# Query, key and value projection by seven block products of eight, with the gate kept in device memory

## The chip, the cores and the metric

The kernel runs on one core of one Trainium2 chip. The metric is the time of one execution on the device in microseconds (us). The kernel before takes 1717.29 us, the median of 3 runs (1715.92 to 1720.21). One execution was recorded by the hardware profiler, and its span is 1717.7 us; all durations below come from that execution.

The engines of a core run their own instruction streams in order: PE (TensorE) multiplies matrices, DVE (VectorE) and ACT (ScalarE) work on rows of numbers, POOL (GpSimd) does odd jobs, SP (SyncE) here only issues transfers between device memory and the core's memory (DMA). An instruction waits where it stands for what it needs, and all behind it on its engine wait with it.

## The reference

Two layers over 512 tokens of width 2048, each with a normalisation in front that is modulated by a conditioning vector, a gate by that vector behind, and a residual sum. Layer 0 mixes tokens by windowed means; layer 1 is sparse attention. What the change touches is layer 1:

```
proj = h @ w_in                                  # (512, 2048) @ (2048, ...)
q, k, v, gate, qi, ki, wi = split(proj)          # q, k, v, gate: 16 heads x 128
q, k = rope(q), rope(k)                          # the first 32 of each head's 128
sel = top_k(relu(qi . ki) weighted by wi, 128)   # keys kept for each query, causal
p = softmax(q . k / sqrt(128), over sel)
out = ((p @ v) * silu(gate)) @ w_out
```

All is float32. For that accuracy each matrix product is made of three products of shorter floats: an operand is split into a high part (hi, wh) and the rest (lo, wl), and hi·wh + hi·wl + lo·wh is summed.

## The kernel before

Layer 1 goes through four stages. The index projection (weights `widx`) gives qi, ki and wi; the gate projection (`wgate`) gives the gate, and in the same stretch DVE finds the top 128 keys; then come 16 heads one after the other with `wqkv`; then the output projection (`wout1`), the residual sum and the last norm.

Weights come in units of two blocks of 128 rows. `unit()` issues the load on SP (L130, 3 buffers `st`), ACT makes the high part `wh` from it (L132), and DVE subtracts to get the rest `wl` (L134), which is the last reading of the buffer. Units are made some steps ahead of use. Two helpers multiply: `gemm_t` (L177 to L179, weights stationary, 512 columns of tokens) and `gemm_n` (L199 to L201, tokens stationary, the weights' 384 columns of one head's q, k and v streaming).

The loop over heads (L732 to L737) makes for each head 8 units x 4 token tiles x 2 blocks x 3 products = 192 matmuls of 384 columns. ACT copies the four results out of PSUM into `nat` (L735). The attention of a head is cut into items (`head_items`): rotation of q and k, transposes and splits of q and k, four rows of logits with a running maximum on DVE (L697), exp on ACT (L700), normalising on DVE (L701, L702), transposes and splits of p, and p @ v with the gate multiplied in (L727). These items wait in a queue `bg`; `step()` takes some after each weight unit of the next head, so that PE never runs out of work. A scheduler settles the order of each engine from the order of the code and its own estimates, and the order is fixed at build time.

The silu of the gate stays in the core's memory as 16 tiles `y` (L651). After the last head `y_split` splits them for the output projection. In the middle of the output projection `cond_rows` runs a second time (L242 to L250): it loads the conditioning row, spreads it over 128 partitions by four matmuls with a column of ones in plain float32 (L248), and ACT takes silu of it (L249) into `cb`; DVE multiplies it with rows of `modT` (L212) for the layer's gate.

Of the kernel before, what the change touches and what calls it, by code (L numbers as in the profile page):

```python
# [17 lines left out]
D = 2048  # L18
# [16 lines left out]
NC = 1  # L35
TWO_PI = 6.283185307179586
# [15 lines left out]
def trunk(ctx, tc, xT, cols, crow, pos, modT, win, wgrp, wout0, widx, wgate, wqkv, wout1, out):  # L52
# [5 lines left out]
    wp = ctx.enter_context(tc.tile_pool(name="wp", bufs=2))  # L58
    tp = ctx.enter_context(tc.tile_pool(name="tp", bufs=1))
    dp = ctx.enter_context(tc.tile_pool(name="dp", bufs=1, space=DRAM))  # L60
    ps = ctx.enter_context(tc.tile_pool(name="ps", bufs=1, space=PSUM))
    turn = [0]

    def bank4():
        return ps.tile([128, 512], F32, name="acc", tag="acc", bufs=4)

    def att():
        return ps.tile([128, 512], F32, name="att", tag="att", bufs=3)

    def misc():  # L70
        return ps.tile([128, 512], F32, name="misc", tag="misc", bufs=1)
# [5 lines left out]
    def tmp(shape=(128, 528)):  # L77
        return tp.tile(list(shape), F32, name="tmp", tag="tmp", bufs=4)

# [12 lines left out]
    acc = cp.tile([128, T], F32, name="acc")  # L92
    rbc = cp.tile([128, T], F32, name="rbc")
# [34 lines left out]
    def unit(src, w):  # L128
        st = wp.tile([128, 2, w], F32, name="st", tag="st", bufs=3)
# [7 lines left out]
    # every weight unit in the order of use; units are split ahead of their use  # L137
# [9 lines left out]
    plan += [(wqkv[h, kp], 384) for h in range(HEADS) for kp in range(8)]  # L147
    plan += [(wout1[c, kp], 512) for c in (0, 1, 2, 3, 3) for kp in range(8)]
# [14 lines left out]
    # out^T[m] (4 column tiles) += W[k, m]^T r[k], weights stationary  # L163
# [22 lines left out]
    # natural-layout projection: out[t, cols] for the given row tiles  # L186
# [66 lines left out]
    def norm_r(t0, t1):  # L253
        nb = (t1 - t0) // 128
        p = misc()
        for j in range(nb):
            mm(p[:, j:j + 1], acc[:, t0 + j * 128:t0 + j * 128 + 128], ones[:, 0:1], start=True, stop=True)
        s = tp.tile([128, 4, 4], F32, name="nrm", tag="nrm", bufs=2)
# [285 lines left out]
    for tt, o in early:  # L544
        n = o.shape[-1]
        nc.scalar.copy(inat[:, tt, 0:n], o)
# [304 lines left out]
```

## Time and profile before

| quantity | value |
|---|---|
| median of 3 runs | 1717.29 us |
| span of the profiled execution | 1717.7 us |
| PE busy | 1684.1 us, 98% of the span |
| DVE busy | 1098.1 us, 64% |
| ACT busy | 642.3 us, 37% |
| POOL busy | 23.9 us, 1% |
| read from and written to device memory | 283.74 MB, 8.39 MB |
| mean granted TensorE clock | 0.996 |

A busy share is the part of the span in which an engine had an instruction under way. The profile's text gives one line for a group of instructions with the line of the program, the engine, what is written and what is read, and the mean length of one. A timeline gives a start and a length of each; the time from one start to the next on the same engine is its pitch, which can be shorter than the length, since the end of an instruction overlaps with the start of the next.

### The profile page before, as it was taken

How to read it: one execution, taken by the hardware profiler on the slowest of the kernel's cores; microseconds unless marked ns; L12 is line 12 of the kernel's file. 1: busy time of each engine (PE TensorE's matmuls, PEld its weight loads, DVE VectorE, ACT ScalarE, POOL GpSimd, SP SyncE). 2: the span in 40 equal slices, each digit the busy share in tenths (PEclk: the TensorE clock that was granted, in tenths of full speed). 3: DMA queues.
4: the chain of work that ended last, by engine and by line, in shares of the span. 5: the costliest groups of instructions: out<-in, count | busy, mean ns of one | idle time of the engine just before them, and what ended most of it. 6: DMA issues, size and time to landing. Idle time of an engine off the chain costs nothing.

```text
span 1717.7 us, 23658 instructions
## 1 busy us (share of the span) xinstructions
PE 1684.1 (98%) x9284; PEld 1531.4 (89%) x9284; DVE 1098.1 (64%) x1867; ACT 642.3 (37%) x1024; POOL 23.9 (1%) x130
## 2 busy tenths in 40 slices
PE   4999999999999999999999999999999999999998
PEld 3888888888889999988889999999999999987897
DVE  6899998999855784566943444444444444554954
ACT  4622221344224563444223333333333333543334
POOL 1000000000000000110000000000000000000000
PEclk9999999999999999999999999999999999999999
DMA  8888988544867865432222222222222222226955
GB/s 327 319 302 308 332 331 324 185 145 172 322 206 249 248 213 172 148 99 74 96 88 88 80 83 83 83 76 81 83 78 81 82 83 83 85 86 226 354 185 178
DMA packets 82772, 293.68 MB, mean 171 GB/s; under 512 B 9314, under 2 KB 17634, under 8 KB 70370
## 3 DMA queue, kind: packets, MB, share of 16 engines
q1 hardware_dynamic: 82660, 292.17, 49.9%
q8 instruction: 73, 1.20, 0.3%
q14 instruction: 39, 0.32, 0.1%
HBM read 283.74 MB, written 8.39 MB: 170 GB/s over the span
## 4 chain that ended last, share of the span: by engine, by line
issue 89%; PE 9%; POOL 1%; DVE 1%; DMA 0%; ACT 0%; POOLq 0%; DVEq 0%; ACTq 0%; SPq 0%
PE acc L177 1%; PE acc L179 1%; PE acc L178 1%; PE acc L200 1%; PE acc L199 1%; PE acc L201 1%; PE att L199 1%; PE att L200 1%; PE att L201 1%; PE att L609 0%; PE att L610 0%; PE misc L583 0%; DVE wl L134 0%; DMA st<-widx 0%; DVE tmp L293 0%
## 5 line engine op out<-in xcount | busy, mean ns | idle before, releaser
L132 ACT CAST wh<-st 128x1024 fp32r<-128x1024 f32 (+2 forms) x360 | 342.9, 953 | 835.7 <-PE acc L178 319.8
L134 DVE TENSOR_TENSOR wl<-st,wh 128x1024 fp32r<-128x1024 f32 (+2 forms) x360 | 396.6, 1102 | 342.4 <-ACT wh L132 336.9
L199 PE MATMUL acc<-wh,hi 128*128 128x384 f32 (+2 forms) x1120 | 381.6, 341 | 0.0
L201 PE MATMUL acc<-wh,lo 128*128 128x384 f32 (+2 forms) x1120 | 373.7, 334 | 0.0
L200 PE MATMUL acc<-wl,hi 128*128 128x384 f32 (+2 forms) x1120 | 373.3, 333 | 0.0
L177 PE MATMUL acc<-hi,wh 128*128 128x512 f32 (+1 forms) x842 | 310.0, 369 | 0.0
L178 PE MATMUL acc<-lo,wh 128*128 128x512 f32 (+1 forms) x842 | 309.5, 368 | 0.0
L179 PE MATMUL acc<-hi,wl 128*128 128x512 f32 (+1 forms) x842 | 309.2, 367 | 0.0
L212 DVE SCALAR_TENSOR_TENSOR ms<-ms,cb 128x2048 f32<-128x2048 f32 x96 | 218.9, 2285 | 23.0 <-ACT cb L249 12.3
L199 PEld LDWEIGHTS acc<-wh,hi 128*128 128x128 f32 x1120 | 210.6, 188 | 0.6
L200 PEld LDWEIGHTS acc<-wl,hi 128*128 128x128 f32 x1120 | 210.7, 188 | 0.3 <-DVE wl L134 0.2
L201 PEld LDWEIGHTS acc<-wh,lo 128*128 128x128 f32 x1120 | 210.3, 188 | 0.0
L178 PEld LDWEIGHTS acc<-lo,wh 128*128 128x128 f32 x842 | 158.9, 189 | 26.6
L177 PEld LDWEIGHTS acc<-hi,wh 128*128 128x128 f32 x842 | 159.1, 189 | 26.4
L179 PEld LDWEIGHTS acc<-hi,wl 128*128 128x128 f32 x842 | 158.8, 189 | 26.4 <-DVE wl L134 0.4
L177 PE MATMUL att<-hi,wh 128*128 128x512 f32 (+1 forms) x374 | 138.3, 371 | 2.2 <-ACT hi L298 2.2
L178 PE MATMUL att<-lo,wh 128*128 128x512 f32 (+1 forms) x374 | 138.4, 370 | 0.0
L179 PE MATMUL att<-hi,wl 128*128 128x512 f32 (+1 forms) x374 | 138.3, 370 | 0.0
L697 DVE CUSTOM_DVE_ANT_0 lg<-att,mbias 128x256 f32<-128x256 f32 (+2 forms) x48 | 26.8, 558 | 95.2 <-PE att L694 95.2
L177 PEld LDWEIGHTS att<-hi,wh 128*128 128x128 f32 x374 | 70.9, 190 | 16.2 <-ACT hi L298 2.6
L178 PEld LDWEIGHTS att<-lo,wh 128*128 128x128 f32 x374 | 71.2, 190 | 12.5 <-DVE lo L299 0.8
L179 PEld LDWEIGHTS att<-hi,wl 128*128 128x128 f32 x374 | 71.3, 191 | 11.6
(208 smaller groups left out, 1969.4 us busy)
## 6 DMA issues: line engine op xcount, KB each, us to landing
ms<-modT SPq DMA_DIRECT2D x96, 1024.0 KB, 7.0
st<-wqkv SPq DMA_DIRECT2D x128, 384.0 KB, 3.0
st<-wout SPq DMA_DIRECT2D x88, 512.0 KB, 4.2
st<-win SPq DMA_DIRECT2D x64, 512.0 KB, 5.1
st<-wgate SPq DMA_DIRECT2D x40, 512.0 KB, 3.5
st<-widx SPq DMA_DIRECT2D x32, 368.0 KB, 3.3
x<-xT SPq DMA_DIRECT2D x16, 256.0 KB, 5.5
st<-wgrp SPq DMA_DIRECT2D x8, 512.0 KB, 3.5
```

Of the source, the lines that this page charges most:

```text
L132: nc.scalar.copy(wh, st)
L134: nc.vector.tensor_tensor(wl, st, wh.bitcast(F32), op=OP.subtract)
L177: mm(o, wh[:, kk, ms], rh[:, t0:t1], start=first, stop=False)
L178: mm(o, wh[:, kk, ms], rl[:, t0:t1], start=False, stop=False)
L179: mm(o, wl[:, kk, ms], rh[:, t0:t1], start=False, stop=last)
L199: mm(o, hi[:, ts], wh[:, kk, 0:n], start=kp == 0 and kk == 0, stop=False)
L200: mm(o, hi[:, ts], wl[:, kk, 0:n], start=False, stop=False)
L201: mm(o, lo[:, ts], wh[:, kk, 0:n], start=False, stop=kp == 7 and kk == 1)
L212: nc.vector.scalar_tensor_tensor(st, st, 1.0, cell["cb"], op0=OP.mult, op1=OP.mult, accum_out=dst)
L697: nc.vector.tensor_tensor_reduce(out=lg, in0=o, in1=mbias[qb], scale=1.0, scalar=GONE, op0=OP.add, op1=OP.max, accum_out=st[:, 0:1])
```

## The change

For a pair of heads a = 2j and b = 2j+1 the product of tokens and weights is cut into 2 x 2 x 2 blocks: token halves (256 each), halves of the depth (1024 each), and the two heads. The eight block products become seven, after Strassen, in Winograd's form, with sums of blocks on both sides. Each product takes four slots; a slot has one unit of weights, two token tiles and 12 matmuls. A pair has 28 slots with 336 matmuls, where it had 384. The order in a pair is P1, P5, P6 four times in turn, then P3, P7 four times, then P2, P4 four times (`qplan`).

The sums on the token side are made once: S1, S2 and S4 by `s_item` (8 items, which the scheduler places in the index projection's stretch), S3 by `s3_item` in place in the first slots of the first pair. The sums on the weights' side are made for each pair by DVE (`q_unit`): 16 more subtractions of 128 x 768 in a pair. The loads have four buffers `qst` and are issued 2 units ahead of the split, which is 3 slots ahead of use; a pair has 24 loads, where it had 16, since head b's eight blocks are loaded twice (for P5 and P7, and for P6 and P3). The results leave PSUM by ACT for P1 and P2, and by 10 additions of 128 x 384 a pair on DVE for the other products.

The attention items are 11 per head now and one is taken per slot; q, k and v tiles have one buffer each. Head 14's items run in the first part of the output projection. The memory for the sums is found by writing each gate tile to device memory (`yd`), reading it back per head (`yg`), writing the product back for heads 0 to 13, and reading that for `y_split`. The second `cb` comes by one transfer that repeats the row on all partitions.

```diff
+QLOOK = 3
+QST = 4
+QAHEAD = 2
...
-    plan += [(wqkv[h, kp], 384) for h in range(HEADS) for kp in range(8)]
-    plan += [(wout1[c, kp], 512) for c in (0, 1, 2, 3, 3) for kp in range(8)]
...
+    yd = dp.tile([KT, 128, T], F32, name="yd")
...
+    HK = KT // 2
+    SS = {(i, k): (sp.tile([128, 256], F32R, name=f"s{i}h{k}"), sp.tile([128, 256], F32R, name=f"s{i}l{k}"))
+          for i in (1, 2, 4) for k in range(HK)}
+
+    def whole(dst, k):
+        hi, lo = hT[k]
+        nc.vector.tensor_tensor(dst, hi.bitcast(F32), lo.bitcast(F32), op=OP.add)
+
+    def s_item(k):
+        def run():
+            ha = yp.tile([128, T], F32, name="ha")
+            hb = yp.tile([128, T], F32, name="hb")
+            whole(ha, k)
+            whole(hb, k + HK)
+            s1, s2, s4 = (yp.tile([128, 256], F32, name=f"sf{i}") for i in (1, 2, 4))
+            nc.vector.tensor_tensor(s1, ha[:, 256:T], hb[:, 256:T], op=OP.add)
+            nc.vector.tensor_tensor(s2, s1, ha[:, 0:256], op=OP.subtract)
+            nc.vector.tensor_tensor(s4, hb[:, 0:256], s2, op=OP.subtract)
+            for i, t in ((1, s1), (2, s2), (4, s4)):
+                split(*SS[i, k], t)
+        return run
+
+    bg.extend(s_item(k) for k in range(HK))
...
+                y_tile(mt)
             nc.scalar.activation(y[mt][:, t0:T], o, AF.Silu)
+            nc.sync.dma_start(yd[mt], y[mt])
...
+    qplan = []
+    for j in range(HEADS // 2):
+        a, b = 2 * j, 2 * j + 1
+        for kp in range(4):
+            qplan += [("P1", kp, (a, kp)), ("P5", kp, (b, kp)), ("P6", kp, (b, 4 + kp))]
+        for kp in range(4):
+            qplan += [("P3", kp, (b, 4 + kp)), ("P7", kp, (b, kp))]
+        for kp in range(4):
+            qplan += [("P2", kp, (a, 4 + kp)), ("P4", kp, None)]
...
+    def q_loads(n):
+        while qpos[0] < min(n, len(qplan)):
+            src = qplan[qpos[0]][2]
+            if src:
+                st = wq.tile([128, 2, QW], F32, name="qst", tag="qst", bufs=QST)
+                nc.sync.dma_start(st, wqkv[src[0], src[1]])
+                qraw[qpos[0]] = st
+            qpos[0] += 1
+
+    def q_unit():
+        i = qpos[1]
+        qpos[1] += 1
+        q_loads(i + 1 + QAHEAD)
+        prod, kp, _ = qplan[i]
+        st = qraw.pop(i, None)
+        sub = lambda o, x, z: nc.vector.tensor_tensor(o, x, z, op=OP.subtract)
+        if prod == "P5":
+            sub(st, st, was["b11"])
+        elif prod == "P6":
+            t2[kp] = wq.tile([128, 2, QW], F32, name=f"t2_{kp}")
+            sub(t2[kp], st, was["t1"])
+            st = t2[kp]
+        elif prod == "P7":
+            sub(st, was["b22"], st)
+        elif prod == "P4":
+            sub(t2[kp], was["b21"], t2[kp])
+            st = t2[kp]
+        keep = {"P1": "b11", "P5": "t1", "P3": "b22", "P2": "b21"}.get(prod)
+        if keep:
+            was[keep] = st
+        wh = wq.tile([128, 2, QW], F32R, name="qwh", tag="qwh", bufs=QLOOK + 1)
+        wl = wq.tile([128, 2, QW], F32R, name="qwl", tag="qwl", bufs=QLOOK + 1)
+        split(wh, wl, st)
+        qready.append((wh, wl))
...
+    def q_slot(prod, kp, banks, wh, wl):
+        opens = prod in ("P1", "P5", "P6")
+        for tt in range(2):
+            o = banks[role[prod]][tt][:, 0:QW]
+            for kk in range(2):
+                hi, lo = lhs(prod, 2 * kp + kk, tt)
+                first = opens and kp == 0 and kk == 0
+                last = kp == 3 and kk == 1
+                mm(o, hi, wh[:, kk, :], start=first, stop=False, skip_group_check=not opens)
+                mm(o, hi, wl[:, kk, :], start=False, stop=False, skip_group_check=not opens)
+                mm(o, lo, wh[:, kk, :], start=False, stop=last, skip_group_check=not opens)
...
+    def s3_item(k):
+        def run():
+            ha = ap.tile([128, T], F32, name="lg", tag="lg", bufs=3)
+            whole(ha, k)
+            nc.vector.tensor_tensor(ha[:, 0:256], ha[:, 0:256], ha[:, 256:T], op=OP.subtract)
+            hi, lo = hT[k]
+            split(hi[:, 256:T], lo[:, 256:T], ha[:, 0:256])
+        return run
+
+    bg.extend(s3_item(k) for k in range(HK))
...
+            cell["y"] = ap.tile([128, T], F32, name="yg", tag="yg", bufs=2)
+            nc.sync.dma_start(cell["y"], yd[h])
...
+            nc.vector.tensor_tensor(cell["y"], o, cell["y"], op=OP.mult)
+            y[h] = cell["y"]
+            if h < HEADS - 2:
+                nc.sync.dma_start(yd[h], cell["y"])
...
-    for h in range(HEADS):
-        nat = ap.tile([128, 4, 384], F32, name="nat", tag="nat", bufs=1)
-        gemm_n(384, (0, 1, 2, 3), bank4,
-               lambda tt, o, nat=nat: nc.scalar.copy(nat[:, tt, :], o), nstep=1)
-        drain()
-        bg.extend(head_items(h, nat))
...
     def y_split(k):
+        src = y[k]
+        if k < HEADS - 2:
+            src = ap.tile([128, T], F32, name="yr", tag="lg", bufs=3)
+            nc.sync.dma_start(src, yd[k])
         yT[k] = hslots(k)
-        split(yT[k][0], yT[k][1], y[k])
-
-    for k in range(KT - 1):
-        y_split(k)
-    bg.append(lambda: y_split(KT - 1))
+        split(yT[k][0], yT[k][1], src)
...
+    for j in range(HEADS // 2):
+        a, b = 2 * j, 2 * j + 1
+        banks = {}
+        na = nb = None
+        for u in range(28):
+            while len(qready) < QLOOK + 1 and qpos[1] < len(qplan):
+                q_unit()
+            wh, wl = qready.popleft()
+            prod, kp, _ = qplan[28 * j + u]
+            if role[prod] not in banks:
+                r = role[prod]
+                banks[r] = [P["ps"].tile([128, 512], F32, name="b" + r, tag="b" + r, bufs=2) for _ in range(2)]
+            q_slot(prod, kp, banks, wh, wl)
+            if kp == 3:
+                B = [t[:, 0:QW] for t in banks[role[prod]]]
+                if prod == "P1":
+                    na = ap.tile([128, 4, QW], F32, name="na", tag="na")
+                    nb = ap.tile([128, 4, QW], F32, name="nb", tag="nb")
+                for tt in range(2):
+                    if prod == "P1":
+                        nc.scalar.copy(na[:, tt, :], B[tt])
+                        nc.scalar.copy(na[:, 2 + tt, :], B[tt])
+                    elif prod == "P5":
+                        ev(nb[:, 2 + tt, :], B[tt], na[:, tt, :], op=OP.add)
+                    elif prod == "P6":
+                        ev(nb[:, tt, :], B[tt], na[:, tt, :], op=OP.add)
+                    elif prod == "P3":
+                        ev(nb[:, tt, :], B[tt], nb[:, tt, :], op=OP.add)
+                    elif prod == "P7":
+                        ev(nb[:, 2 + tt, :], B[tt], nb[:, 2 + tt, :], op=OP.add)
+                    elif prod == "P2":
+                        nc.scalar.copy(na[:, tt, :], B[tt])
+                    else:
+                        ev(na[:, 2 + tt, :], B[tt], na[:, 2 + tt, :], op=OP.add)
+                if prod == "P7":
+                    bg.extend(head_items(b, nb))
+                    if j == HEADS // 2 - 1:
+                        hot.extend(lambda k=k: y_split(k) for k in range(HK))
+                elif prod == "P4":
+                    bg.extend(head_items(a, na))
+            step(1)
+    while hot:
+        hot.popleft()()
+    hot.extend(lambda k=k: y_split(k) for k in range(HK, HEADS - 2))
+    for k in (HEADS - 2, HEADS - 1):
+        bg.append(lambda k=k: y_split(k))
...
-    gemm_t(range(8), lambda k: yT[k], bank4, lambda m, o: early.append((m, o)), nstep=2)
+    gemm_t(range(8), lambda k: yT[k], bank4, lambda m, o: early.append((m, o)), nstep=2.6, nhot=2, mid={6: drain})
...
-    bg.append(lambda: cond_rows(op_, lambda: op_.tile([1, D], F32, name="cr", tag="ms", bufs=3)))
+    cell["cb"] = op_.tile([128, D], F32, name="cb")
+    nc.sync.dma_start(cell["cb"], crow.to_broadcast([128, D]))
+    nc.scalar.activation(cell["cb"], cell["cb"], AF.Silu)
```

The first place is DVE in the stretch of a head's logits. Before, with `wl` the rest of a weight unit, `lg` the logits of one row block and `stt` its maximum and sum:

```order
L134 TENSOR_TENSOR wl_9793<-st_9789,wh_9791 128x768
L161 TENSOR_TENSOR ql_9771<-att_9765,qh_9770 128x512
L161 TENSOR_TENSOR kl_9780<-att_9774,kh_9779 128x512
L697 ISA lg_9823,stt_9824<-att_9819,dmask_5868 128x128
L697 ISA stt_9824 128x1
L134 TENSOR_TENSOR wl_9834<-st_9830,wh_9832 128x768
L699 TENSOR_SCALAR stt_9824<-stt_9824 128x1
```

And now, in a pair in the middle, with `qwl` the rest of a unit, `qst` a loaded unit and `t2` a sum of units:

```order
L177 TENSOR_TENSOR qwl_10256<-qst_10201,qwh_10255 128x768
L760 TENSOR_TENSOR qst_10332<-qst_10332,qst_10305 128x768
L177 TENSOR_TENSOR ql_10250<-att_10244,qh_10249 128x512
L177 TENSOR_TENSOR qwl_10282<-t2_2_9844,qwh_10281 128x768
L177 TENSOR_TENSOR kl_10277<-att_10271,kh_10276 128x512
L760 TENSOR_TENSOR t2_0_10434<-qst_10362,qst_10332 128x768
L177 TENSOR_TENSOR qwl_10308<-qst_10253,qwh_10307 128x768
L854 ISA lg_10327,stt_10328<-att_10323,dmask_5869 128x128
L854 ISA stt_10328 128x1
L177 TENSOR_TENSOR qwl_10336<-t2_3_9929,qwh_10335 128x768
L856 TENSOR_SCALAR stt_10328<-stt_10328 128x1
```

Between the split of q and the maximum of the first logits there stood nothing but k's split; now two splits of units and one difference of units stand there too, and the difference reads `qst_10362`, a load that has to be in place by then.

The second place is SP between the gate's stage and the heads. Before:

```order
L130 DMA st_7882<-wgate 128x1024
L130 DMA st_7918<-wgate 128x1024
L130 DMA st_7956<-wqkv 128x768
L130 DMA st_7992<-wqkv 128x768
L130 DMA st_8040<-wqkv 128x768
```

And now, with `yst` a gate tile in the core and `yd` the gate in device memory:

```order
L712 DMA yd_114<-yst_8185 128x512
L712 DMA yd_114<-yst_8194 128x512
L712 DMA yd_114<-yst_8203 128x512
L842 DMA yg_8771<-yd_114 128x512
L712 DMA yd_114<-yst_8212 128x512
L842 DMA yg_9102<-yd_114 128x512
L750 DMA qst_8234<-wqkv 128x768
L750 DMA qst_8236<-wqkv 128x768
```

The first loads for the heads stood in the queue right behind the last of the gate's weights; now they stand behind the writes of the gate's last four tiles. `qst_8234` takes the memory of earlier tiles and waits, among others, for the write of `yst_8203`.

The third place is PE in the output projection. Before, with `cr` the conditioning row and `ones` the column of ones:

```order
L178 MATMUL acc_14143<-lo1_13678,wh_14033 128x512
L179 MATMUL acc_14143<-hi1_13677,wl_14035 128x512
L248 MATMUL acc_14153<-cr_14150,ones_73 128x512
L248 MATMUL acc_14156<-cr_14150,ones_73 128x512
L248 MATMUL att_14159<-cr_14150,ones_73 128x512
L177 MATMUL att_14122<-hi2_13681,wh_14063 128x512
```

A part of the difference between the two streams on PE:

```order
-L248 MATMUL acc<-cr,ones 128x512 x3
-L248 MATMUL att<-cr,ones 128x512
```

The four matmuls with the column of ones are gone there; SP has one transfer `cb<-crow` in their stead, between loads of `wout1`.

## Rows read from the trace of the kernel before

**Rows 1.** Busy time by stretch: PE, PEld, DVE, ACT, POOL, clock, DMA share, GB/s.

```profile
890.00:1510.00 620.00, 620.00 (x3699) 613.20 (x3697) 272.34 (x625) 228.39 (x434) 0.00 (x0) 1.00 0.27 83
```

**Rows 2.** Timeline of ACT, heads' results: start, length, line, written and read.

```profile
995.92 0.48 ACT L735 COPY nat<-acc 128x384 f32<-128x384 f32 x1
...
1035.10 0.48 ACT L735 COPY nat<-acc 128x384 f32<-128x384 f32 x1
```

**Rows 3.** Timeline of PE from the gate into the heads.

```profile
888.88 0.39 PE L179 MATMUL acc<-hi,wl 128*128 128x512 f32 x1
889.10 0.33 PE L199 MATMUL acc<-wh,hi 128*128 128x384 f32 x1
...
891.21 0.33 PE L199 MATMUL acc<-wh,hi 128*128 128x384 f32 x1
...
892.94 0.33 PE L200 MATMUL acc<-wl,hi 128*128 128x384 f32 x1
```

**Rows 4.** Timeline of PE in the output projection.

```profile
1565.05 0.39 PE L179 MATMUL acc<-hi,wl 128*128 128x512 f32 x1
1565.37 1.98 PE L248 MATMUL acc<-cr,ones 1*128 1x512 f32 x4
1567.19 1.02 PE L248 MATMUL att<-cr,ones 1*128 1x512 f32 x2
...
1570.45 2.07 PE L248 MATMUL att<-cr,ones 1*128 1x512 f32 x2
...
1576.10 0.40 PE L177 MATMUL acc<-hi,wh 128*128 128x512 f32 x1
```

**Rows 5.** Busy time by stretch, the output projection around them.

```profile
1568.00:1572.00 4.00, 4.00 (x9) 1.85 (x8) 0.00 (x0) 1.18 (x3) 0.00 (x0) 0.60 0.46 131
1572.00:1576.00 4.00, 4.00 (x10) 2.83 (x10) 2.82 (x3) 0.60 (x1) 0.00 (x0) 0.54 0.63 186
```

**Rows 6.** Timeline of DVE in a head; a bracket is idle time before.

```profile
1001.51 0.69 DVE L727 TENSOR_TENSOR y<-misc,y 128x512 f32<-128x512 f32 x1
1002.11 0.68 DVE L161 TENSOR_TENSOR vl<-nat,vh 128x512 fp32r<-128x512 f32 x1
1005.98 0.96 DVE L134 TENSOR_TENSOR wl<-st,wh 128x768 fp32r<-128x768 f32 x1 [3.19 <-ACT wh L132]
1006.86 0.68 DVE L161 TENSOR_TENSOR ql<-att,qh 128x512 fp32r<-128x512 f32 x1
```

**Rows 7.** Groups of DVE by shape, ten heads: count, busy us, mean ns, idle before.

```profile
L134 DVE TENSOR_TENSOR wl<-st,wh 128x768 fp32r<-128x768 f32 x80 | 76.5, 956 | 93.0 <-ACT wh L132 91.8
L161 DVE TENSOR_TENSOR pl<-att,ph 128x384 fp32r<-128x384 f32 x10 | 5.5, 551 | 0.0
```

**Rows 8.** Busy time by stretch: ten heads, full DVE, index stage, around it.

```profile
1000.00:1391.70 391.70, 391.70 (x2342) 387.16 (x2341) 170.13 (x401) 140.09 (x271) 0.00 (x0) 1.00 0.27 81
100.00:200.00 100.00, 100.00 (x443) 82.80 (x442) 98.93 (x130) 26.24 (x28) 0.00 (x0) 1.00 0.86 312
640.00:664.00 24.00, 23.95 (x152) 23.78 (x152) 13.34 (x18) 10.98 (x16) 0.00 (x0) 1.00 0.75 206
595.00:690.00 95.00, 92.58 (x656) 92.01 (x655) 62.30 (x106) 49.39 (x81) 2.28 (x6) 1.00 0.64 193
```

**Rows 9.** DMA issues of the page: KB each, median us from issue to landing.

```profile
st<-wqkv SPq DMA_DIRECT2D x128, 384.0 KB, 3.0
...
st<-widx SPq DMA_DIRECT2D x32, 368.0 KB, 3.3
```

**Rows 10.** DMA issues in the stretch 480 to 640, a write.

```profile
x1d<-tmp SPq DMA_DIRECT2D x5, 256.0 KB, 3.5
```

**Rows 11.** Timeline of ACT from the gate into the heads.

```profile
887.94 0.60 ACT L651 ACTIVATE y<-acc 128x512 f32<-128x512 f32 x1 [0.76 <-PE acc L179]
...
889.82 0.59 ACT L651 ACTIVATE y<-acc 128x512 f32<-128x512 f32 x1
```

More of the change, by code (lines that the diff above doesn't have):

```diff
@@ L77, in tmp @@
     def tmp(shape=(128, 528)):
-        return tp.tile(list(shape), F32, name="tmp", tag="tmp", bufs=4)
+        return P["tp"].tile(list(shape), F32, name="tmp", tag="tmp", bufs=4)
     cl = cp.tile([128, 160], F32, name="cl")
@@ new lines, in trunk @@
+    wq = er.enter_context(tc.tile_pool(name="wq", bufs=1, side="right", reuse_waits="tile"))
+    eq = ExitStack()
+    P["ps"] = eq.enter_context(tc.tile_pool(name="pq", bufs=1, space=PSUM, reuse_waits="tile"))
+    P["natt"] = 2
+    qplan = []
[7 more added lines that the diff above has]
+            qplan += [("P2", kp, (a, 4 + kp)), ("P4", kp, None)]
@@ L706, in trans @@
[L706 to L716 removed]
+            n = (qb + 1) * 128
@@ new lines, in soft @@
+            (qh, ql), (kh, kl) = cell["q"], cell["k"]
+            o = att()[:, 0:n]
+            qs = slice(qb * 128, qb * 128 + 128)
+            mm(o, qh[:, qs], kh[:, 0:n], start=True, stop=False)
+            mm(o, qh[:, qs], kl[:, 0:n], start=False, stop=False)
+            mm(o, ql[:, qs], kh[:, 0:n], start=False, stop=True)
+            lg = ap.tile([128, n], F32, name="lg", tag="lg", bufs=3)
+            st = ap.tile([128, 4], F32, name="stt", tag="stt", bufs=6)
+            nc.vector.tensor_tensor_reduce(out=lg, in0=o, in1=mbias[qb], scale=1.0, scalar=GONE,
+                                           op0=OP.add, op1=OP.max, accum_out=st[:, 0:1])
@@ L728, in head_items @@
[L728 to L737 removed]
+                ph, pl = cell["ph"][:, sb, r], cell["pl"][:, sb, r]
@@ new lines, in pvs, with at, run @@
+                mm(o[:, r], vh[:, sb, :], ph, start=sb == 0, stop=False)
+                mm(o[:, r], vh[:, sb, :], pl, start=False, stop=False)
+                mm(o[:, r], vl[:, sb, :], ph, start=False, stop=sb == 3)
+            nc.vector.tensor_tensor(cell["y"], o, cell["y"], op=OP.mult)
+            y[h] = cell["y"]
+            if h < HEADS - 2:
+                nc.sync.dma_start(yd[h], cell["y"])
+        def at(*fs):
+            def run():
+                for f, *args in fs:
+                    f(*args)
+            return run
@@ new lines, in trunk @@
+    while hot:
[3 more added lines that the diff above has]
+        bg.append(lambda k=k: y_split(k))
+    early = []
+    er.close()
+    eq.close()
+    ctx.enter_context(open_banks())
+    ctx.enter_context(open_work("right"))
+    plan += [(wout1[c, kp], 512) for c in (0, 1, 2, 3, 3) for kp in range(8)]
+    gemm_t(range(8), lambda k: yT[k], bank4, lambda m, o: early.append((m, o)), nstep=2.6, nhot=2, mid={6: drain})
```

188 lines of the change are left out of this document (102 added, 86 removed).

## The prediction

> **What bounds the kernel now.** I read the busy shares by stretch first. In the heads' stretch PE is busy without a gap, DVE for 272 of 620 us and ACT for 228, and the transfers take 0.27 of the DMA engines [rows 1]. So PE sets the time there; the reader should see that DVE has 348 us of slack, the resource on which the change draws. Second, the timelines give PE's unit of work. Head results leave PSUM at 995.92 and 1035.10, so a head takes 39.18 us and a pair 78.35 [rows 2]. From 891.21 to 892.94 there are ten starts of matmuls of 384 columns, 0.1736 us each (the heads' whole stretch gives the fourth digit); a matmul of 512 columns takes 0.226 [rows 3]. The 192 matmuls of a head are 33.3 us, and the attention matmuls the other 5.85. Third, outside the heads one hole stands on PE: the ones-matmuls in the output projection [rows 4].
>
> **Work taken from PE.** A pair has 336 matmuls for 384, so 48 x 8 = 384 matmuls go, and 384 x 0.1736 = 66.7 us. Bare, a pair then takes 336 x 0.1736 = 58.3, and with twice 5.85 of attention 70.0 us. The matmuls are of the same shape, so this term is certain if PE stays the bound.
>
> **The conditioning row by transfer.** Between 1565.28 (a matmul's pitch after 1565.05) and 1576.10 stand the four ones-matmuls and 15 ordinary ones [rows 4]. [...] Now ACT makes silu in one instruction of 2048 columns and a table load, as long as the four pieces before; if the row's transfer is late behind weights, ACT's casts behind it wait and up to 3 us come back. I take -7.4, bounds -4 and -8.
>
> **Token sums in the index projection.** Each of the 8 items has two additions of 512 columns and six operations of 256 columns. The pitch of a 512 operation on DVE is 0.60 (1001.51 to 1002.11) and of a 768 one 0.88 [rows 6]; a line through the two gives 0.32 for 256. An item is 1.2 + 1.95, 8 items 25 us. In 95 us of that stretch DVE is busy 62.3 [rows 8], so 33 are free, but the units there run with transfers at 206 GB/s and a unit every 1.85 us, and a rest that comes late holds PE. That DVE at 98.9% need not hold PE is seen elsewhere in the same trace [rows 8]. I take +4, bounds 0 and +10.
>
> **From the gate into the heads.** Before, no gap: the first matmul of the heads starts 0.22 us after the gate's last [rows 3], because their first loads stood ahead. Now they stand behind the writes of the gate tiles, and the first of them waits for the write of the tile whose silu runs from 887.94 to 888.54 [rows 11]. A write of 256 KB takes 3.5 us [rows 10], a load of 384 KB 3.0 [rows 9]: 888.6 + 3.5 + 3.0 = 895.1, then the cast (0.84) and the rest (0.96), so PE starts at about 896.5 instead of 889.1. That is 7.4; the first products want a unit each 2.1 us from a pipeline that just starts, and PE may run at the lower clock after the pause as it did in [rows 5]: +2. I take +9.5, bounds +5 and +13. The eight sums S3 (one operation of 512 and two of 256 columns, 1.24 us of DVE each) fall into this hole.
>
> **The steady pairs.** This is the term that decides. DVE's work in a pair: 28 rests and 16 differences of weights, 44 x 0.88 = 38.7; 10 additions of 384 columns, by their length of 0.551 [rows 7] less the overlap of 0.08 about 0.48, so 4.8; and the attention of two heads. For ten heads DVE is busy 170.1 us [rows 8], of which 76.5 are rests [rows 7]; 9.4 per head is left, and I take 9.5 since rests overlap with their neighbours. Together 38.7 + 4.8 + 19 = 62.5 us, 89% of PE's 70.0. That fits if nothing waits. But the loads have four buffers, two of which the sums keep for longer. From the order I added up the DVE work between its last reading of a buffer and its first use of the load that refills it: for 14 of the 24 loads of a pair it is 1.5 to 3.2 us, while the refill takes 3.0 [rows 9] and about 0.2 to be released and issued. The shortfalls add to 12 us; some hide one another, so some 10 us of waiting on a transfer per pair. DVE would be occupied 72.5 of PE's 70.0. It is not even: cut at the first logits of b, the first logits of a and the additions of P3, where DVE must have work from PE, DVE with waits has 32.1, 31.0 and under 11.5 us, and PE 29.0, 29.5 and 11.5. The sum of the longer is 74.6. The excess over 70.0 is 4.6 to 4.7, for 7 pairs +33 (the first pair is in the term above). On SP the load of the next gate tile waits for the write of the product in the same buffer (3.5 us) with loads of weights behind it; I count that within the 10 us, as it falls once or twice a pair on a load already late. Bounds: 0, if every refill is early enough, and +71 (below).
>
> **The end.** In the last pair the splits for the output projection come on DVE on top, 8 x 0.6 and their reloads: +3. Head 14's attention runs in the output projection, whose matmuls are the same as before plus these: they move, they are not added; +1 for its waits on one unit. The loads of the weights for `wout1` start only when the heads' memory is free; I count that in these 4.
>
> **The sum** against the profiled execution: 1717.7 - 66.7 - 7.4 + 4 + 9.5 + 33 + 4 = 1694.1 us. The execution is 0.4 above the median of the runs, so the forecast is 1694.
>
> **Rivals.** (1) *PE stays the bound.* If the refills take 2.6 us or the three slots of units made ahead absorb the waits, a pair is 70 to 71 us and the 33 become 0 to 7: 1661 to 1668. For it: transfers take a quarter of the DMA engines [rows 1], and DVE's shortfalls are each under 1.7 us, less than a slot of 2.5. Against it: the 89% of DVE leaves only 7.5 us to catch up, less than the 10 us of shortfalls.
>
> (2) *DVE becomes the bound and the kernel gets slower.* The mechanism is the length of DVE's operations: if each occupied DVE for its whole length (0.956, not 0.88), the pair would need 62.5 x 1.087 = 68 us, and with the 10 us of waits and 2 for the unevenness 80: 10.1 x 7 = 71 in place of 33, so 1732. It decides from a pair of about 78 us on, where the excess of 8 x 7 eats the other gains. Against it the trace: after a rest of 0.96 us at 1005.98 the next operation starts at 1006.86, 0.08 before the recorded end [rows 6], and this is what happens at every pair of neighbours I looked at. [...] The same loss would come of attention's round trips from PE over DVE and ACT, which now queue behind up to two more operations each of 0.9 us; nothing in the trace shows how much of that PE can hide.
>
> (3) *Transfers slower, and no difference.* Per pair 24 loads and four gate tiles pass, 10.5 MB in 75 us, 140 GB/s against 83 now [rows 1]. At 206 GB/s [rows 8] the index loads, smaller ones, take 3.3 [rows 9]. With 0.5 us more per refill the 14 short loads lack 7 us more, of which half would show, a pair takes 78 and the time is 1717: the gain is eaten up.
>
> **Chances.** The forecast's own mechanism, DVE partly late, 1670 to 1711: 0.46. Rival 1, below 1670: 0.27. Rival 3, within 0.3% of before (1712 to 1722; that is about what a measurement of this kernel can tell from no change): 0.10. Rival 2, above 1722: 0.17. That makes 0.73 faster, 0.10 same, 0.17 slower. The range reaches over rival 1 to 1656 and up to rival 2's 1732, leaving some 0.15 outside; 1670 to 1711 is the likeliest case's own.
>
> **What would show it.** In the profile after, the pairs should be some 75 us apart, seen at the additions of P3 or the maxima of the first logits; DVE near 85% busy in the stretch with idle time on `qwl` or the differences, ended by transfers of `qst`; PE with some 4 us of idle time a pair. A hole of 7 us on PE should stand at the start of the heads, and none at the conditioning row. Pairs at 70 us with PE gapless make rival 1 right; pairs above 78 with DVE gapless rival 2; pairs of 78 with loads of 3.5 us and more rival 3. A hole of 15 us or more at one of the changes of stage, or a layer 0 that runs otherwise than before, would make the prediction wrong in a way that I did not see.

## The result and the profile after

The changed kernel takes 1692.27 us (median of 4 runs, 1689.19 to 1693.65) where the kernel before took 1718.75 in the same session: a ratio of 0.9846, 95% interval 0.983 to 0.9862. The forecast was 1694. Medians here leave out two runs whose mean granted clock was low: one of the kernel before (1864.74 us at 0.851) and one of the kernel without differences (2019.06 us at 0.755). The profiled execution's span is 1689.4 us against 1717.7, 28.3 less. From the page of the changed kernel, busy times first, then a group of DVE's instructions and a transfer:

```profile
PE 1626.4 (96%) x8892; PEld 1461.7 (87%) x8892; DVE 1358.0 (80%) x2260; ACT 717.6 (42%) x1133; POOL 24.3 (1%) x130
...
L760 DVE TENSOR_TENSOR qst<-qst 128x768 f32<-128x768 f32 x64 | 61.1, 955 | 38.0 <-DMA qst<-wqkv 38.0
...
qst<-wqkv SPq DMA_DIRECT2D x192, 384.0 KB, 3.2
```

PE was busy to 98% before and is now to 96% of a shorter span; DVE rose from 64% to 80%. `qst` is the load, which takes 3.2 us where it took 3.0 [rows 9]; the differences of weights (L760) are what waits for it.

Seven pairs lie between the additions of P3 in the first and in the last pair. Timeline of DVE, and busy times of that stretch (columns as in [rows 1]) with the index projection's beside it:

```profile
940.18 1.01 DVE L936 TENSOR_TENSOR nb<-bz,nb 128x384 f32<-128x384 f32 x2
...
1455.80 1.01 DVE L936 TENSOR_TENSOR nb<-bz,nb 128x384 f32<-128x384 f32 x2
```

```profile
595.00:690.00 95.00, 93.00 (x660) 92.60 (x659) 87.14 (x171) 57.18 (x105) 1.79 (x4) 1.00 0.59 184
940.18:1455.80 515.62, 498.69 (x2941) 480.94 (x2940) 435.07 (x831) 255.50 (x454) 0.00 (x0) 1.00 0.47 147
```

A pair takes 515.62 / 7 = 73.66 us where two heads took 78.35 [rows 2]. PE is idle 16.9 us of it, 2.4 a pair; DVE is busy 435.07 / 7 = 62.2 a pair. In the index projection DVE went from 62 of 95 us [rows 8] to 87, and PE did not slow down: its last gate matmul starts at 887.95, where it was 888.88 [rows 3].

The waits in the pairs, engine and waiting line, what it waited for, us in total, times, longest; first DVE, then PE:

```profile
DVE qst L760 <- DMA qst<-wqkv: 35.6, 35, 1.9
DVE t L760 <- DMA qst<-wqkv: 25.3, 34, 2.0
```

```profile
PE att L869 <- DVE lg L863: 6.8, 14, 0.8
PE att L825 <- DVE nb L546: 4.9, 7, 0.9
PE att L849 <- DVE stt L854: 2.9, 7, 0.6
```

DVE stands 60.9 us, 8.7 a pair, before differences whose load has not landed. PE never waits for a split of weights there; it waits for the attention's own operations on DVE (normalised logits, rotation, a maximum whose reading frees a PSUM tile) and once, 1.2 us, for an addition of results. These stand among and behind the differences in DVE's order.

The start of the heads, first on SP, then on PE, then the busy times of that stretch:

```profile
889.00 0.32 SPq L712 DMA_DIRECT2D yd<-yst  x1
...
891.63 8.56 SPq L750 DMA_DIRECT2D qst<-wqkv  x7
```

```profile
887.95 0.39 PE L195 MATMUL acc<-hi,wl 128*128 128x512 f32 x1
895.96 1.01 PE L802 MATMUL bx<-qwh,hi 128*128 128x384 f32 x2 [7.62 <-ACT qwh L176]
...
901.60 0.52 PE L803 MATMUL bz<-qwl,s1h 128*128 128x384 f32 x1
```

```profile
895.96:902.24 6.28, 6.28 (x19) 5.79 (x19) 6.28 (x9) 2.66 (x4) 0.00 (x0) 0.50 0.69 233
```

The granted clock is 0.50 there, where PE had stood idle for 7.62 us before, and 1.00 in the seven pairs. Eighteen matmuls start in these 6.28 us, the first three 0.49 us apart and the others 0.32, where 0.1736 is the usual pitch. (The 19 in the row counts the one that starts at 902.24.)

### The profile page after: what moved, and what is told of

Read it like the earlier page. It is cut to its first block, busy times and chain, and to the rows that moved or that the text cites. A ratio compares the mean times of both kernels' runs of the same rounds, so it can differ in the third digit from the quotient of the medians.

```text
span 1689.4 us, 23722 instructions
## 1 busy us (share of the span) xinstructions
PE 1626.4 (96%) x8892; PEld 1461.7 (87%) x8892; DVE 1358.0 (80%) x2260; ACT 717.6 (42%) x1133; POOL 24.3 (1%) x130
## 4 chain that ended last, share of the span: by engine, by line
PE 48%; issue 24%; DVE 15%; DMA 11%; ACT 1%; POOL 1%; DVEq 0%; POOLq 0%; SPq 0%; ACTq 0%
DMA qst<-wqkv 10%; PE acc L195 8%; PE acc L193 8%; PE acc L194 8%; DVE qwl L177 6%; PE att L195 4%; PE att L193 4%; PE att L194 4%; DVE t L760 2%; DVE qst L760 1%; PE acc L216 1%; PE acc L215 1%; PE acc L217 1%; PE by L804 1%; PE by L803 1%
## 5 line engine op out<-in xcount | busy, mean ns | idle before, releaser
L150 ACT CAST wh<-st 128x1024 fp32r<-128x1024 f32 (+1 forms) x232 | 236.2, 1018 | 497.4 <-PE acc L194 289.0
L152 DVE TENSOR_TENSOR wl<-st,wh 128x1024 fp32r<-128x1024 f32 (+1 forms) x232 | 273.9, 1181 | 137.1 <-ACT wh L150 135.1
L194 PE MATMUL acc<-lo,wh 128*128 128x512 f32 (+1 forms) x810 | 299.2, 369 | 0.0
L176 ACT CAST qwh<-qst 128x768 fp32r<-128x768 f32 x160 | 133.6, 835 | 137.9 <-PE by L804 47.8
L177 DVE TENSOR_TENSOR qwl<-qst,qwh 128x768 fp32r<-128x768 f32 x160 | 151.4, 950 | 10.6 <-ACT qwh L176 10.5
L802 PE MATMUL bx<-qwh,hi 128*128 128x384 f32 x256 | 89.5, 351 | 7.6 <-ACT qwh L176 7.6
L760 DVE TENSOR_TENSOR qst<-qst 128x768 f32<-128x768 f32 x64 | 61.1, 955 | 38.0 <-DMA qst<-wqkv 38.0
L802 PE MATMUL by<-qwh,hi 128*128 128x384 f32 x256 | 87.3, 341 | 1.3 <-DVE nb L938 1.2
L195 PEld LDWEIGHTS att<-hi,wl 128*128 128x128 f32 x406 | 76.7, 189 | 12.4
L803 PE MATMUL bx<-qwl,hi 128*128 128x384 f32 x256 | 87.0, 340 | 0.0
L804 PE MATMUL bx<-qwh,lo 128*128 128x384 f32 x256 | 86.8, 339 | 0.0
```

The costliest lines, as they stand in the source:

```text
L150: nc.scalar.copy(wh, st)
L152: nc.vector.tensor_tensor(wl, st, wh.bitcast(F32), op=OP.subtract)
L176: nc.scalar.copy(hi, src)
L177: nc.vector.tensor_tensor(lo, src, hi.bitcast(F32), op=OP.subtract)
L194: mm(o, wh[:, kk, ms], rl[:, t0:t1], start=False, stop=False)
L195: mm(o, wl[:, kk, ms], rh[:, t0:t1], start=False, stop=last)
```

## The experiments

Each ran in a session with the kernel before, and each ratio is to that kernel in the same session. Pair lengths are read from the additions of P3 as above, waits from the same stretch.

**The conditioning row alone** (on the kernel before).

```diff
-    bg.append(lambda: cond_rows(op_, ...))
+    cell["cb"] = op_.tile([128, D], F32, name="cb")
+    nc.sync.dma_start(cell["cb"], crow.to_broadcast([128, D]))
+    nc.scalar.activation(cell["cb"], cell["cb"], AF.Silu)
```

> The kernel before with one part of the change alone: the second conditioning row comes by a transfer that repeats it on all partitions, and the four ones-matmuls of the output projection are gone. Theory (the prediction's term): the whole hole of 7.4 us around 1565 to 1576 goes, the ordinary matmuls there run at 0.226 us each, and the time falls by 7.4 us, to about 1711. Rival: the transfer or ACT's silu of 2048 columns comes late and holds ACT's casts, so that a hole of 3 us or more takes the place of the old one and the time falls by 0 to 4 us.

Measured: 1713.56 against 1717.27, ratio 0.9975 (0.9965 to 0.9986), which is 4.3 us; the profiled span is 1711.0, 6.7 less. The stretch that had 9 and 10 matmuls in 4 us [rows 5] has its 19 and 20 at full clock:

```profile
1568.00:1572.00 4.00, 4.00 (x19) 3.33 (x18) 3.42 (x5) 3.44 (x5) 0.00 (x0) 1.00 0.98 372
1572.00:1576.00 4.00, 4.00 (x20) 3.30 (x19) 2.56 (x4) 0.54 (x1) 0.00 (x0) 1.00 0.81 276
```

The hole goes wholly, as the theory says, but the timed runs show 2.4 to 6.0 us of it, not 7.4. The granted clock suggests why. Of eleven executions of the kernel before that were timed beside it, the seven with a mean clock of 0.998 or 0.999 took 1716.0 to 1718.2 us, and the four with 0.996 or 0.997 took 1718.5 to 1721.0. The profiled one has 0.996. So the 7.4 seems to hold for executions in which the clock falls behind the ones-matmuls (granted 0.60 and 0.54 in [rows 5]), with some 3 us less at stake in the others; no profile of one of the others was kept, so this is not shown.

**Weight units at the upper end of memory** (on the kernel before).

```diff
-    wp = ctx.enter_context(tc.tile_pool(name="wp", bufs=2))
+    wp = ctx.enter_context(tc.tile_pool(name="wp", bufs=2, side="right"))
```

> The kernel before with one thing changed: the pool of weight units (st, wh, wl) lies at the upper end of the core's memory for the whole program, as it does after the change in the output projection alone. There a matmul of 512 columns was started each 0.2333 us after the change and each 0.2266 before, one of 256 columns each 0.1178 and 0.1200. Theory: the pitch follows from where the stationary weights lie, so all 3264 matmuls of 512 columns take 0.0067 us more and 1536 of 256 columns 0.0022 less: +18 us where PE sets the time, to about 1730 to 1736. Rival: the pitch follows from something else in the output projection of the changed kernel (its transfers, its PSUM tiles, the order), and the time stays within 3 us of 1717 with a pitch of 0.2266.

Measured: 1733.9 against 1717.27, ratio 1.0092 (1.0076 to 1.0108), some 16 us more. PE's timeline in this kernel, then in the changed one, then in the kernel before:

```profile
1620.05 0.40 PE L177 MATMUL att<-hi,wh 128*128 128x512 f32 x1
...
1620.75 0.39 PE L177 MATMUL att<-hi,wh 128*128 128x512 f32 x1
```

```profile
1570.67 0.40 PE L193 MATMUL att<-hi,wh 128*128 128x512 f32 x1
...
1571.38 0.39 PE L193 MATMUL att<-hi,wh 128*128 128x512 f32 x1
```

```profile
1600.61 0.39 PE L177 MATMUL att<-hi,wh 128*128 128x512 f32 x1
...
1601.29 0.39 PE L177 MATMUL att<-hi,wh 128*128 128x512 f32 x1
```

Each time the second line is the third matmul after the first. The first two kernels have a pitch of 0.233 us, as expected by the theory, and the kernel before 0.227. In the built programs the tokens of these matmuls lie at 9 to 73 KB of a partition in both this kernel and the one before, and the weights go from 85 to 109 KB up to 199 to 223: so with the place of the weights this pitch went from 0.227 to 0.233 us. A pitch near the longer one is also seen with the weights where they were: layer 0 of the kernel before has matmuls whose tokens (`yh`, `yl`) lie at 121 KB and above, with the weights still at 85 to 109, and they start 0.232 us apart:

```profile
470.12 0.40 PE L177 MATMUL att<-yh,wh 128*128 128x512 f32 x1
...
470.82 0.40 PE L177 MATMUL att<-yh,wh 128*128 128x512 f32 x1
```

In the changed kernel the output projection alone has its weights there, and its 576 matmuls of 512 columns cost 576 x 0.0067 = 3.9 us more, its 384 of 256 columns 0.8 less: 3.0 us.

**No differences of weights.**

```diff
-        sub = lambda o, x, z: nc.vector.tensor_tensor(o, x, z, op=OP.subtract)
+        sub = lambda o, x, z: None
...
-            sub(t2[kp], st, was["t1"])
-            st = t2[kp]
+            t2[kp] = st
...
-            sub(t2[kp], was["b21"], t2[kp])
-            st = t2[kp]
+            st = was["b21"]
```

> The changed kernel with the 16 subtractions of weights per pair left out (products are made of the loaded blocks alone, so the result is not the reference's); loads, casts, rests, matmuls and additions stay. DVE has 14.1 us less of 62 in a pair, and no operation of DVE reads a load before ACT has. Theory: PE's 2.4 us of waits per pair come of DVE being late with the attention's operations, so they go: pair 70.3 to 71.3 for 73.66, and the time 1668 to 1676. Rival (the attention's round trip over ACT, or PE's own work, makes the pair): pair 73 or more, time 1688 or more.

Measured: 1663.51, ratio 0.9689 (0.9667 to 0.9711), below the theory's range; pairs of 70.38 us, within it, PE without a gap over seven of them:

```profile
937.95:1430.62 492.67, 492.67 (x2942) 482.38 (x2942) 349.54 (x721) 257.20 (x454) 0.00 (x0) 1.00 0.48 153
```

So the bare pair is 70.4, where the prediction had 70.0, and all of the other 3.3 us comes of the differences, by their work or by their waits. Of the 3.3 us 2.4 are PE's idle time; the other 0.9 lies in its busy time (498.69 / 7 = 71.2 us a pair). The stretch behind the last pair is shorter too, 229.6 us from P3's last addition for 233.6.

**Five buffers, and its control.** The fifth buffer's memory comes from the rotation's small tiles, which share those of k's split; the control has that alone.

```diff
-QST = 4
-QAHEAD = 2
+QST = 5
+QAHEAD = 3
...
-            rope(ap, "rh", x[:, :, 0:2, 0:32], cosa, sina, ...)
+            # the same four operations on halves of tiles with the tags kh and kl
```

> The changed kernel with five buffers for loaded weights in place of four, and loads issued 3 units ahead for 2; the memory comes from the rotation's two small tiles, which share the tiles of k's split. DVE's work is the same. Theory of the prediction (refills of 3.2 us come too late, and what DVE loses so, 8.7 us a pair, makes PE wait): DVE's waits for transfers fall to 3 us a pair or less, PE's waits to under 1.2, pair 71.5 to 72.5, time 1676 to 1685. Rival (DVE is late because 62 us of work in order is too much, transfers or not): waits for transfers fall but the pair stays within 0.5 of 73.66 and the time within 4 us of 1692.

> Control for the run with five buffers: the changed kernel with four buffers as it is, and only the rotation's two small tiles put into the tiles of k's split. Theory (the fifth buffer gave the 15 us): time within 3 us of 1692, pair 73.2 to 74.1. Rival (the gain came of the scheduler's other order or of the tiles' places): 1677 to 1685.

Measured: 1677.54, ratio 0.9766 (0.975 to 0.9781); the control 1691.16, 0.9841 (0.9823 to 0.9858). The waits fell to 5.9 us a pair, not to 3, and the pair to 72.55:

```profile
DVE qst L760 <- DMA qst<-wqkv: 24.0, 25, 2.5
DVE t L760 <- DMA qst<-wqkv: 17.4, 24, 1.7
```

The seven pairs account for 7.8 us of the two profiles' difference of 14.0; 4.4 more lie behind the last pair and 1.8 ahead of the first. The control keeps the time of the changed kernel, so the gain is not that of the tiles' places.

**Three buffers** in place of four.

```diff
-QST = 4
-QAHEAD = 2
+QST = 3
+QAHEAD = 1
```

> The changed kernel with three buffers for loaded weights in place of four, and loads issued one unit ahead. Theory (the pairs are held by refills that come late; one buffer more took DVE's waits for transfers from 8.7 to 5.9 us a pair and 14 us from the time): the waits go up to 15 to 25 us a pair, DVE is occupied for 78 to 86 us, the pairs are 78 to 86 us long and the time is 1722 to 1780: the change would lose its gain for want of 3 KB a partition. Rival (the order, not the refill): pair under 75, time under 1700.

Measured: 1672.82, ratio 0.9732 (0.9716 to 0.9749): faster than with four, by some 19 us, where the theory had it slower by 30 and more. Waits for loads are 2.1 us a pair, the pair is 71.84:

```profile
DVE qwl L177 <- ACT qwh L176: 32.6, 43, 1.0
DVE qst L760 <- DMA qst<-wqkv: 11.3, 15, 1.5
...
DVE t L760 <- DMA qst<-wqkv: 3.2, 6, 0.9
```

The loads are no faster (3.4 us at the median, 3.2 with four buffers), and one buffer less gives a load no more time by itself. What differs is the order, in which DVE now waits 4.7 us a pair for ACT's casts where it waited 1.3. DVE's order around b's first logits with three buffers, to be held against the second piece of order shown ahead of the prediction:

```order
L760 TENSOR_TENSOR qst_10360<-qst_10360,qst_10330 128x768
L177 TENSOR_TENSOR qwl_10306<-qst_10278,qwh_10305 128x768
L854 ISA lg_10325,stt_10326<-att_10321,dmask_5869 128x128
L854 ISA stt_10326 128x1
L177 TENSOR_TENSOR qwl_10334<-t2_3_9927,qwh_10333 128x768
L856 TENSOR_SCALAR stt_10326<-stt_10326 128x1
L862 RECIPROCAL stt_10326<-stt_10326 128x1
L863 TENSOR_SCALAR lg_10325<-lg_10325,stt_10326 128x128
L854 ISA lg_10353,stt_10354<-att_10349,mbias1_5874 128x256
L854 ISA stt_10354 128x1
L760 TENSOR_TENSOR t2_0_10432<-qst_10393,qst_10360 128x768
```

`t2_0`, the difference for the next pair's first P6, stood ahead of the first logits with four buffers and now stands behind the second ones; DVE does the attention's work while the load is under way. The prediction's own measure, summed again from each order (DVE work between the last reading of a buffer and the first use of its refill, short of 3.2 us), goes with the waits, whatever the number of buffers; the first column has the median of the seven pairs of each trace:

| kernel | shortfall a pair, from the order | DVE waits for loads, a pair | PE waits, a pair | pair |
|---|---|---|---|---|
| changed kernel, 4 buffers | 12.4 | 8.7 | 2.4 | 73.66 |
| control | 12.5 | 8.7 | 2.7 | 73.75 |
| 4, other reloads | 12.4 | 8.5 | 2.0 | 73.18 |
| 4, no writing back | 12.4 | 8.4 | 2.2 | 73.22 |
| 4, early loads | 10.8 | 6.6 | 2.6 | 74.23 |
| 5 | 9.0 | 5.9 | 1.5 | 72.55 |
| 5, all three | 8.4 | 4.2 | 1.0 | 71.70 |
| 3 | 5.5 | 2.1 | 0.8 | 71.84 |
| 7, all three | 5.9 | 3.9 | 0.9 | 71.50 |
| 7, without early loads | 5.9 | 3.3 | 1.1 | 71.59 |
| no differences | - | 0.0 | 0.0 | 70.38 |

It does not go in step: at 5.5 to 5.9 of shortfall the waits are 2.1 to 3.9, and with seven buffers and all three the pairs' own sums range from 4.0 to 9.4. With three buffers DVE is busy 62.9 us a pair, no less than with four, and the pair is 1.8 us shorter; so at least that much of the 3.3 us goes with the waits and the order, not with the work of the differences.

The order and the release were not changed apart from each other in any run, and the number of buffers always together with how far ahead loads are issued; so how much each has in the waits stays open.

**Early first loads.** Two of the four buffers get memory of their own in the gate's stage; `s_item`'s scratch goes to shared tiles for it; `t2` is allocated first.

```diff
+        if c == 3:
+            for src in ((0, 0), (1, 0)):
+                st = wq0.tile([128, 2, 384], F32, name="qst", tag="qsa", bufs=2)
+                nc.sync.dma_start(st, wqkv[src[0], src[1]])
...
-            nc.sync.dma_start(yd[mt], y[mt])
+            (nc.scalar if c == 3 else nc.sync).dma_start(yd[mt], y[mt])
```

> The changed kernel with the first two loads of the heads moved ahead: two of the four buffers have their own memory from the gate's stage on (the token sums' scratch shares other tiles for it), their loads are issued before the gate's last chunk, the last four gate tiles are written by ACT's queue in place of SP's, and the sums of weights take the place in memory that the buffers had. Theory (the first load waits behind the write of a gate tile): PE's hole of 7.6 us at the start of the heads falls to 2 to 4, the third load being the next limit, and the time by 4 to 6 us, to 1686 to 1688. Rival (DVE's and ACT's chain of the eight S3 sums fills the hole anyway): the hole stays above 6 us and the time above 1690.

Measured: 1690.76, ratio 0.9842 (0.9826 to 0.9858). The hole shrank as expected, but the time is in the rival's range, and the gate's end came 2.5 us later:

```profile
890.47 0.39 PE L195 MATMUL acc<-hi,wl 128*128 128x512 f32 x1
893.39 0.76 PE L819 MATMUL bx<-qwh,hi 128*128 128x384 f32 x2 [2.53 <-ACT qwh L176]
```

P3's first addition comes at 935.60, 4.6 us earlier than in the changed kernel, and its last at 1455.18, 0.6 earlier: with pairs of 74.23 the gain was given back. One of its pairs is 77.02 us long: PE waits in it for an addition of results, and the granted clock is 0.50 soon after:

```profile
1161.90 0.42 PE L819 MATMUL by<-qwh,hi 128*128 128x384 f32 x1 [1.92 <-DVE nb L955]
```

```profile
1163.37:1166.78 3.41, 3.03 (x13) 2.47 (x13) 3.26 (x8) 0.99 (x3) 0.00 (x0) 0.50 0.11 37
```

The other six are 73.76 us in the mean. That they are no shorter than in the changed kernel, with 2 us a pair fewer waits of DVE for loads, is the one row of the table that doesn't fit, and is not explained.

**Reloads at the end.**

```diff
-            src = ap.tile([128, T], F32, name="yr", tag="lg", bufs=3)
+            src = wq.tile([128, 2, QW], F32, name="yr", tag="qst", ...) if k < HK else <as before>
...
-... nstep=2.6, nhot=2, mid={6: drain})
+... nstep=2.6, nhot=1, mid={6: drain})
```

> The changed kernel with the reloads of the spilled products for the output projection made earlier: the first eight go through the four free weight buffers in place of the three logits tiles, and the other six are taken one per step in place of two. Theory (ACT's casts of reloaded tiles stand in order before the cast of p, wait for their transfers, and hold PE for 2.5 us, after which the clock is lower for 2 us): the hole at 1486 goes and the time falls by 3 to 5 us, to 1687 to 1689. Rival (the tail's loss is in the matmuls' pitch alone): 1691 to 1693.

Measured: 1688.1, ratio 0.9828 (0.981 to 0.9847), within the theory's numbers, but not by its mechanism: the hole on PE is still there, 2.68 us at 1488.83, and the stretch behind P3's last addition is 2.8 us longer than in the changed kernel. The pairs were 73.18; the gain is no more than the pairs differ between kernels that should have the same, and by the intervals it can't be told from none. In the changed kernel the hole is this (ACT, then PE):

```profile
1486.25 0.62 ACT L176 CAST hi<-yr 128x512 fp32r<-128x512 f32 x1 [1.85 <-DMA yr<-yd]
1486.78 1.04 ACT L150 CAST wh<-st 128x1024 fp32r<-128x1024 f32 x1
1487.72 0.58 ACT L176 CAST ph<-att 128x512 fp32r<-128x512 f32 x1
```

```profile
1485.58 0.40 PE L195 MATMUL acc<-hi,wl 128*128 128x512 f32 x1
1488.35 0.50 PE L880 MATMUL att<-ph,vh 128*128 128x512 f32 x1 [2.38 <-ACT ph L176]
```

**No writing back.**

```diff
-            if h < HEADS - 2:
-                nc.sync.dma_start(yd[h], cell["y"])
```

> The changed kernel without the writing back of the gated heads (the output projection reads the gate alone back, so the result is not the reference's); the reload of a head's gate then waits for no write, and SP isn't held 28 us in all. Theory (this hold is part of the late refills, once or twice a pair): DVE's waits for transfers fall by 1 to 3 us a pair, pair 72 to 73, time 1680 to 1688. Rival (the held loads had time to spare): pair 73.4 to 74, time 1689 to 1694.

Measured: 1686.75, ratio 0.9811 (0.9794 to 0.9827). The waits are 8.4 us a pair and the pair 73.22: SP's wait for the write hardly matters for the loads. The time lies in the theory's range, the waits fell less than it said, and the pair is between the two.

**Together.** Five buffers, early loads and the other reloads; then seven buffers with `QAHEAD = 5` and `QLOOK = 2`, with and without the early loads.

> The three together: five buffers, early first loads, other reloads at the end. Theory (three separate losses that add): 1677.5 less 5 less 3, so 1668 to 1672. Rival (they overlap, or the early loads' memory makes other waits): 1674 to 1679.

> Seven buffers for loads, issued 5 units ahead, paid with one unit less of the split units that stand ahead (2 for 3); with early first loads and the other reloads at the end, as in the run with five buffers and all three. Theory (loads are what DVE waits for): its waits for transfers fall from 4 us a pair to under 1 and the pair from 71.7 to 70.4 to 71, time 1662 to 1667. Rival (with 2 units ahead PE meets every late split): pair 72 or more, time above 1671.

> As the run before it, without the early first loads. Theory (the early loads win 5 us at the start of the heads and lose 2.3 in the stretch before, since the sums' scratch is shared): 1665 to 1670, some 3 us more than with them. Rival (what they win is given back in the pairs, as it was with four buffers): within 1 us of that run or below it.

Measured: 1670.98, ratio 0.9728 (0.9713 to 0.9742); 1670.15, 0.9712 (0.9695 to 0.973); 1672.64, 0.9732 (0.9717 to 0.9746). All beat both kernels. The first is as its theory had it. Seven buffers gain nothing that can be told from five: 3.9 us of waits a pair stay, where under 1 was expected, and both times lie above their theories' ranges. The early loads are worth 2.5 us there by the medians, near the 3 of the theory, but the two intervals overlap. Three buffers alone (1672.82) come within 3 us of the best.

## Why the prediction was right, step by step

The forecast of 1694 lies 1.7 us from the median, and that is in part luck. The sum of 1694.1 was worked out against a span, and a time is some 1.8 us longer than the span of the same execution (1691.16 and 1689.4), which the step from the sum to the forecast left out. Span against span the sum is 4.7 us too high, and its terms were off by more, with both signs. Against the profiled executions, whose difference is 28.3:

| term | predicted | measured |
|---|---|---|
| matmuls taken from PE | -66.7 | bare pair 70.4 where 70.0 was said; the 0.4 stands in the pairs' row |
| conditioning row | -7.4 | -6.7 by the profile, -4.3 by the runs |
| token sums | +4 | -0.9 at the gate's end |
| start of the heads | +9.5 | +7.8 for the hole, +3.2 for eighteen matmuls at a granted clock of 0.50 |
| seven pairs | +33 | 7 x (73.66 - 70.0) = +25.6 |
| last pair and output projection | +4 | +9.4, which is what is left |

*The pairs* were right in their parts: DVE busy 62.2 of 62.5 forecast, 8.7 of 10 us of waits for loads. What was mis-sized is how much of it PE sees: PE hid 1 us a pair more, and is idle 2.4 us where some 4 was said. That a pair is longer than its bare length by the differences is shown by the run without them. The mechanism needs one correction, which the run with three buffers forced: the waits go with where the order puts the differences, and fewer buffers can have fewer of them. The prediction read them from the order as built, so its sum held; my expectations for the runs took the order as fixed, and failed there. The 0.2 us for a refill's release and issue were an estimate: in the trace of the kernel before, a rest on DVE ends at 1055.72, and the issue of a refill on SP starts at 1055.75 and takes 0.33.

*The start* has the mechanism that was worked out, a first load that waits for the write of a gate tile: it is issued at 891.63 (892.1 was said), and PE starts at 895.96 (896.5 was said). That the numbers are so near is luck. The write that it waits for last is not that of `yst_8203`, which landed at 889.65, but that of the last tile, issued at 889.00 and landed at 891.57; it stood 1.4 us later in time, and took 2.6 us where 3.5 was said. Also PE starts right behind the cast, without the rest. What was priced at 2, the matmuls behind PE's pause, took 3.2 more than at the usual pitch, at a granted clock of 0.50.

*The conditioning row*: no run shows a gain of 7.4. That is 10.82 us less 15 matmuls of 0.226 [rows 4], in a stretch whose granted clock is 0.50 from 1568.84 to 1575.66; the run with that part alone was 6.7 us shorter by the profile and 4.3 by the runs.

*The token sums* cost nothing that can be seen: with DVE busy for 87 of 95 us PE was busy for 93.00, where it was 92.58 [rows 8], so the lower bound of that term was the right end. The 0.9 us less is no gain either: the last gate matmul starts between 887.67 and 889.51 in kernels that are the same up to there.

*The end* failed. "Head 14's attention runs in the output projection ... +1 for its waits" and +3 for the last pair missed the pitch of the matmuls with the weights at the other end of memory (0.2333 us for 0.2266, 3.0 us in all; the second run shows the pitch), the hole of 2.4 at 1486, and the clock behind it, granted 0.97 from 1480 to 1490 and 0.86 from 1490 to 1500 (1.7 us). The remaining 2 us are spread and not settled. What would remove the hole was not found with the run on the reloads. No pause of 0.8 us or more is left there in the run with all three, nor in that with three buffers, whose reloads are the changed kernel's; so the reloads alone don't make it.

Of the rivals, PE as the bound would have been 1661 to 1668 and is what the run without differences gives (1663.51). DVE's lengths adding up, 68 us a pair without waits, is contradicted by 62.2 busy. Slower transfers: loads took 3.2, not 3.5.

## What to carry to other kernels

When work is moved from PE to an engine in order, sum that engine's work against PE's, and then read its order for what stands ahead of data that isn't there yet: at 84% busy, the differences with 9 us of such waits cost a pair 3. More buffers are not a remedy by themselves: the order is built anew for each number, and here three were faster than four (1672.82 us for 1692.27). That a scheduler which counts on an early load puts its use early would explain it; no run shows that. And a change of pools moves tiles: check the pitch of the untouched matmuls (0.227 to 0.233 us here).

## What the runs showed of the hardware

In the traces of this case the pitch of a float32r matmul differed with where its operands lie in the core's memory; the pitches are from the traces, the places from the built programs. In the output projection of the kernel before, with the tokens at 9 to 73 KB of a partition and the weights at 85 to 109 KB, 512 columns take 0.2266 us and 256 columns 0.1200. In that of the changed kernel, with the tokens at 5 to 69 KB and the weights at 194 to 218 KB, it is 0.2333 and 0.1178. In the kernel before with its weights at 199 to 223 KB and the tokens where they were, 512 columns take 0.233, and the whole kernel some 16 us more (1733.9 for 1717.27). With the weights at 85 to 109 KB and the tokens at 121 KB and above, in layer 0 of the kernel before, it is 0.232 and 0.118. Matmuls of 384 columns with the tokens stationary hardly differed: 0.1738 us in the kernel before, with the weights at 85 to 108 KB, and 0.1740 in the changed one, with them at 134 to 158 KB. What in the hardware makes these differences was not shown.
